# Late modulation blocks in layer 1's mixing, a shorter entry and early zeroing in a two-layer expert-choice transformer kernel

## The chip, the cores and the metric

One core of one Trainium2 chip runs the whole program. The metric is the device time in microseconds (us) of one execution, lower being better; the profiled execution's rows are times from the start of its span.

## The reference, cut to what matters

Two blocks run one behind the other on `x` of 512 tokens by 1024 features; only the first one is touched by the change. It has two layers and carries a second stream of 256 context tokens, `ctx`, that the last layer no longer updates.

```
for i in range(2):
    mods  = silu(c)     @ ada_w[i] + ada_b[i]      # 6 x 1024: sh1, sc1, g1, sh2, sc2, g2
    cmods = silu(c_ctx) @ ada_w[i] + ada_b[i]
    h  = rms_norm(x, n1)  * (1 + sc1) + sh1        # and hc from xc with cmods
    p  = h @ w_in[i]                               # 11 pieces: a_b a_c a_h b_v b_g c_q c_k c_v d_q d_k d_v
    x  = x + g1 * (concat(conv(a), conv31(b), window_attn(c), global_attn(d)) @ w_out[i])
    h2 = rms_norm(x, n2) * (1 + sc2) + sh2
    aff = softmax(h2 @ router)                     # each of 16 experts takes its best 64 (32) tokens
    x  = x + g2 * sum over experts of gate * ((silu(xs @ w_gate) * (xs @ w_up)) @ w_down)
```

All data is float32. A layer's expert weights are 16 x 3 matrices of 1024 x 1024 (4 MB each), its modulation weights `ada_w[i]` 1024 x 6144 (24 MB).

## The kernel before, in words

**Modulation.** `ada_gen` (lines 310 to 332) works `ada_w` off in blocks of 512 output columns, twelve a layer. A block is four loads of 512 KB from the SP queue (`ada_load`, line 191), 8 matmuls into one PSUM bank, a copy on ACT, four transposes, and a reduce and an add on DVE into `M[l]`. Blocks 0 and 1 are sh1, 2 and 3 sc1 (an even block holds features 0 to 511, the odd one the rest), 4 and 5 g1, 6 and 7 sh2, 8 and 9 sc2, 10 and 11 g2. While one block is computed, three or four loads of the next are issued.

**Entry** (lines 211 to 398). The SP queue gets small rows of constants, four loads of `x`, blocks 0, 2, 1 and 3 of layer 0, two loads of `ctx`, and weights for the first dense units. The small rows land in `rows`, are transposed in four groups (`rows_to_cols`, line 347) and become `cols`. Each of six token tiles is squared, transposed and scaled. When all four blocks are there, `norm1_first` (line 387) goes over the eight feature tiles k: ACT makes the rounded part `hh`, DVE the full value and its remainder `hl` (POOL the remainder of the context).

**Dense** (line 419) multiplies with `w_in` and `w_out`: a unit is 128 output columns; its 512 KB of weights are split into a rounded part `wh` (ACT, line 442) and a remainder `wl` (POOL, line 443), and 24 matmuls of 512 columns and, in layer 0, 24 of 256 follow (lines 473, 475), three for each k. The q pieces have their columns regrouped, so `colload2` (line 490) fetches a unit in two loads of 64-column pieces. A unit's weights go through one of five buffers named `raw`, which the modulation loads share. `la` units are loaded ahead, or, with `ahead`, one from a certain unit on.

**Mixing.** `run_all` (lines 944 to 947) weaves four generators: `gd` (18 dense units), `at` (attention), `ga` (modulation blocks) and `cv` (the 31-tap convolution). In layer 0 `ga` makes layer 0's blocks 4 to 11 and layer 1's 0 to 7. In layer 1 it is empty. Attention's rope takes sine and cosine from `tabl`, loaded by POOL's queue (line 638) when the entry's buffers are free.

**Experts** (line 1022). `wload` issues 512 KB weight tiles in the order g0, u0, g1, d0, u1, g2 and so on, into a ring of 25 in layer 0 (18 `rawA`, 5 `raw`, 2 `rawB`). Ahead of layer 0's experts stand the router stage's steps: logits to affinities, writing normalised rows to `hd` in DRAM, eight rounds of max, index and replace on DVE, indices, and the first gathers by POOL (line 1209). Woven into it are layer 1's modulation blocks 8 to 11 (line 1110) and the zeroing of the DRAM sums `sumx` and `sumc` (lines 1134 to 1139). Expert e's outputs are then added to these sums by indirect DMAs, up to e = 13 for x and 11 for the context; the rest goes through one-hot matmuls. Back they come as six tiles `rb` (two buffers), each taken up by two `sums_add` (line 1311) of four transposes and four DVE operations. Context's four stand in expert 15's up product, x's eight in its down product.

**Order.** The code is traced, and a scheduler then orders each engine's instructions by priority, dependencies and free buffers, so the order on an engine is near to the code's, but not the same. Each engine runs its list in order, and so does each DMA queue's issue.

Of the kernel before, what the change touches and what calls it, by code (L numbers as in the profile page):

```python
# [134 lines left out]
def main_kernel(ctx, tc, I, out, stop=None, dbg=None, manual=False):  # L135
# [37 lines left out]
    dx = pool(ctx, "dx", space=DRAM).tile([128, 8 * 768], F32)  # L173
# [44 lines left out]
    rows = ent.tile([128, 4, 128], F32)  # L218
    xin = xip.tile([128, 4, 1024], F32)
    cin = xip.tile([128, 2, 1024], F32)  # L220
    ada0 = ent.tile([128, 4, 4, 1024], F32)
# [20 lines left out]
    x_load(1)  # L242
    row_load(G, 0, "qn", I["q_norm_g"], 2, dup=True)
    row_load(G, 0, "kn", I["k_norm_g"], 2, dup=True)
    row_load(G, 0, "cbb", I["conv_b_b"].rearrange("l (h p) -> (l h) p", p=128), 4)
    row_load(G, 0, "lng", I["conv_ln_g"].rearrange("l (h p) -> (l h) p", p=128), 4)
    row_load(G, 0, "lnb", I["conv_ln_b"].rearrange("l (h p) -> (l h) p", p=128), 4)
# [3 lines left out]
    x_load(2)  # L251
    SY.dma_start(sinkb, bass.AP(tensor=I["sink"].tensor, offset=I["sink"].offset, ap=[[0, 128], [1, 8]]))
    row_load(SY, 0, "fg", I["final_g"].rearrange("(k p) -> k p", p=128), 8)
    row_load(SY, 0, "ln1", I["ln1_2"].rearrange("l (k p) -> (l k) p", p=128), 8)
    x_load(3)
# [3 lines left out]
    ada_load(0, 0, ada0[:, 0], hfs=(0, 1))  # L259
    row_load(SY, 3, "cq", I["conv_qkv_2"].rearrange("l t (h p) -> (l t h) p", p=128), 48)  # L260
    row_load(SY, 3, "fc", I["ffn_conv_2"].rearrange("l t (h p) -> (l t h) p", p=128), 66)
    ada_load(0, 0, ada0[:, 0], hfs=(2, 3))
    ada_load(0, 2, ada0[:, 2])
    for t in range(2):
        SY.dma_start(cin[:, t, :], I["ctx"][0, t * 128:(t + 1) * 128, :])
    ada_load(0, 1, ada0[:, 1])
    pre0 = {}
    pre0[0] = raw_tile().rearrange("p (k c) -> p k c", k=8)
    SY.dma_start(pre0[0], I["w_in"][0, :, 1536:1664].rearrange("(k p) c -> p k c", p=128))
    pre0[1] = raw_tile().rearrange("p (k c) -> p k c", k=8)  # L270
    for h in range(2):
        SY.dma_start(pre0[1][:, :, 64 * h:64 * h + 64],
                     I["w_in"][0, :, 1280 + 128 * h:1344 + 128 * h].rearrange("(k p) c -> p k c", p=128))
    ada_load(0, 3, ada0[:, 3])
# [34 lines left out]
    def ada_gen(l, blocks, pl, psp):  # L309
        g, o, n = RO["adab"]  # L310
        for b in blocks:
# [8 lines left out]
            if 3 < b < 11 or (l == 1 and b != 7 and b < 11):  # L320
                ada_load(l, b + 1, hfs=range(4 if l == 1 and b > 7 else 3))
# [10 lines left out]
            yield  # L332

# [7 lines left out]
    if True:  # L341
        with ExitStack() as e0:
# [4 lines left out]
            def rows_to_cols(g, n):  # L347
                p = pse.tile([128, 512], F32, name="rc")
                T.transpose(p[:, :n], rows[0:n, g, :], ident[0:n, 0:n])
                V.tensor_copy(cols[:, g, 0:n], p[:, :n])  # L350

            rows_to_cols(0, 16)
            A.activation(s2[:, :, 0], col("c"), AF.Silu)
            A.activation(s2[:, :, 1], col("cc"), AF.Silu)
            ga = ada_gen(0, (0, 2, 1, 3), sqp, pse)
            ss = ent.tile([128, 6], F32)
            for t in range(6):
# [16 lines left out]
                if t == 1:  # L374
                    rows_to_cols(1, RO["n", 1])
# [4 lines left out]
            for g in (0, 2, 3):  # L380
                rows_to_cols(g, RO["n", g])
            V.tensor_scalar(nsink, sinkb, -1.0, None, op0=OP.mult)

        entry.close()

        def norm1_first(sqp):
            a1 = sqp.tile([128, 8, 2], F32, name="a1")
            for k in range(8):
# [32 lines left out]
        def dense(units, hh, hl, dw, dps, la=3, pre={}, ahead=None):  # L421
# [5 lines left out]
            def load(i):  # L427
                if i in pre:
                    raw[i] = pre[i]
                elif i < len(units):  # L430
                    raw[i] = raw_tile().rearrange("p (k c) -> p k c", k=8)
                    units[i][0](raw[i])

            def split(i):
                if i < len(units):
                    nk = units[i][4] if len(units[i]) > 3 else 8
                    hi[i] = []
                    for a in range(0, nk, 4):
                        n = min(4, nk - a)
                        wh = dw.tile([128, 4, 128], F32R, name="wh")  # L440
                        wl = dw.tile([128, 4, 128], F32R, name="wl")
                        A.activation(wh[:, :n], raw[i][:, a:a + n], AF.Copy)  # L442
                        G.tensor_tensor(wl[:, :n], raw[i][:, a:a + n], wh[:, :n].bitcast(F32), op=OP.subtract)  # L443
                        hi[i].append((wh, wl))
# [40 lines left out]
        def colload(src, c0, n=128):  # L485
            def f(raw):
                SY.dma_start(raw[:, :, 0:n], src[:, c0:c0 + n].rearrange("(k p) c -> p k c", p=128))
            return f

        def colload2(src, ca, cb):  # L490
            def f(raw):
                for h, c in enumerate((ca, cb)):
                    SY.dma_start(raw[:, :, 64 * h:64 * h + 64], src[:, c:c + 64].rearrange("(k p) c -> p k c", p=128))
            return f
# [107 lines left out]
        def layer(l):  # L602
# [6 lines left out]
            with (es_l0 if has else ExitStack()) as es, ExitStack() as er:  # L609
# [5 lines left out]
                psp = Psum(ps, {"px": 3, "s": 2, "pt": 1, "misc": 1, "y": 1}, {"pc": "px"})  # L615
                if has:

                    hh, hl = hh0, hl0
                    norm1_first(sqp)
# [245 lines left out]
                c0 = dict(a_b=0, a_c=256, a_h=512, b_v=768, b_g=1024, c_q=1280, c_k=1536, c_v=1664,  # L865
                          d_q=1792, d_k=2048, d_v=2176)

                def unit(n, ev, nt=NT, j=0):
                    return (colload(w_in, c0[n] + 128 * j), ev, nt)

                def qunit(n, ev, j):
                    return (colload2(w_in, c0[n] + 64 * j, c0[n] + 128 + 64 * j), ev, NT)

                u_c = [unit("c_k", ev_rope(partial(put_k, kC)), 768)] + \
                      [qunit("c_q", ev_rope(partial(put_q, qC, j)), j) for j in range(2)] + [unit("c_v", ev_v(vC), 768)]
                u_d = [unit("d_k", ev_dk, 768)] + [qunit("d_q", ev_dq(j), j) for j in range(2)] + \
                      [unit("d_v", ev_v(vD), 768)]
                u_b = [unit("b_g", ev_bg(j), j=j) for j in range(2)] + [unit("b_v", ev_bv(j), j=j) for j in range(2)]
                u_a = [unit("a_c", ev_ac(j), j=j) for j in range(2)] + [unit("a_h", ev_ah(j), j=j) for j in range(2)] + \
                      [unit("a_b", ev_ab(j), j=j) for j in range(2)]  # L880
# [52 lines left out]
                ga = iter(())  # L933
                if has:
# [3 lines left out]
                    ga = ada_rest()  # L938

                gd = dense(u_c + u_b + u_d + u_a, hh, hl, dw, psp, pre=pre0 if has else {}, ahead=4 if has else None)  # L940
                at, cv = att_gen(), conv31()
                w1, w2, w3 = (28, 28, 64) if has else (18, 18, 44)
                run_all((dense_part(gd, 12), 12))
                run_all((dense_part(gd, 12), 12), (steps(at, w1), w1), (steps(ga, 8), 8))
                c1 = 16 if has else 8
                run_all((dense_part(gd, 12), 12), (steps(at, w2), w2), (steps(ga, 8), 8), (steps(cv, c1), c1))
                run_all((gd, 18), (at, w3), (ga, 16), (cv, (42 if has else 21) - c1))
# [74 lines left out]
        def experts(l, rwpA, lg, rbias, a2, nA, nB):  # L1022
# [37 lines left out]
            if has:  # L1060
                ada_load(1, 8)
            with ExitStack() as es:
# [4 lines left out]
                if has:  # L1067

                    accs = dr.tile([1024, 512], F32, name="sumx"), dr.tile([1024, 256], F32, name="sumc")
# [16 lines left out]
                with ExitStack() as e2:  # L1086
# [3 lines left out]
                    ga = ada_gen(1, range(8, 12), mp, Psum(ps, {"yx": 1}, {"misc": "yx"})) if has else iter(())  # L1090
# [29 lines left out]
                    for _ in steps(ga, 2):  # L1120
                        pass
# [12 lines left out]
                    if has:  # L1134
                        zz = sqp.tile([128, 1024], F32, name="ht", bufs=4)
                        G.memset(zz, 0.0)
                        for acc_, n in zip(accs, (512, 256)):
# [6 lines left out]
                    for i in range(8):  # L1144
# [5 lines left out]
                        if i in (2, 4, 6):  # L1150
                            for _ in steps(ga, 2):
                                pass
# [827 lines left out]
```

## Time and profile before

| | us |
|---|---|
| median of 3 runs | 2653.49 (2650.05 to 2656.85) |
| the profiled execution | 2657.17 |
| its span, first to last instruction | 2655.0 |

TensorE is busy for 2476.4 us of the span (93%), DVE for 1092.9, ACT for 870.2, POOL for 637.8. The DMA engines are full in two long stretches, the expert stages of the two layers (some 380 to 409 GB/s), and at the entry. Busy TensorE is not TensorE at its peak, and the shares are averages over stages with different limits, so a stage is read by what its waits end on.

### The profile page before, as it was taken

To read this page: it belongs to the slowest core of one execution; us is meant where nothing else is said; L and a number is where in the kernel's file an instruction comes from. 1 tells how busy PE (TensorE), PEld (TensorE's weight loads), DVE (VectorE), ACT (ScalarE), POOL (GpSimd) and SP (SyncE) were. 2 spreads that over 40 slices of the span, in tenths; PEclk is the share of its full clock that TensorE was granted. 3 is DMA by queue.
4 is the path that set the end of the run, shared out by engine and by line. 5 is a ranking of instruction groups with operands and counts; after the bars stand their busy time and mean duration, and the time that the engine had idled before them with its cause. 6 is when DMAs were issued, how large, how long until landed. Compare 5 with 4: busy or idle time off the path is not lost.

```text
span 2655.0 us, 41308 instructions
## 1 busy us (share of the span) xinstructions
PE 2476.4 (93%) x16415; PEld 1500.4 (57%) x16415; DVE 1092.9 (41%) x2371; ACT 870.2 (33%) x1769; POOL 637.8 (24%) x552
## 2 busy tenths in 40 slices
PE   7999999699999999899979989898899999999998
PEld 4766777344444333577753322132577787888886
DVE  4488852311111113689641102021665555444411
ACT  4544362211111110464531111110562435443422
POOL 3533112011111100633220000000333233444443
PEclk8999999899999999799989999999899999999999
DMA  8454455999999998222179999999421102333332
GB/s 281 140 165 139 149 177 197 322 383 385 385 386 385 388 394 313 58 59 52 61 289 386 394 398 399 399 404 409 130 67 32 40 25 64 95 96 96 92 96 67
DMA packets 324758, 584.08 MB, mean 220 GB/s; under 512 B 36864, under 2 KB 190007, under 8 KB 323927
## 3 DMA queue, kind: packets, MB, share of 16 engines
q1 hardware_dynamic: 311943, 555.16, 57.7%
q0 software_dynamic: 12480, 26.23, 4.1%
q8 instruction: 129, 2.11, 0.3%
q14 instruction: 62, 0.51, 0.1%
q10 hardware_dynamic: 144, 0.08, 0.0%
HBM read 556.74 MB, written 18.87 MB: 217 GB/s over the span
## 4 chain that ended last, share of the span: by engine, by line
PE 62%; DMA 21%; DVE 9%; issue 3%; POOL 2%; ACT 1%; SPq 1%; ACTq 0%; DVEq 0%; POOLq 0%
PE px L473 21%; DMA rawA<-in_w_gate_dram 4%; DMA rawA<-in_w_down_dram 4%; PE ax L1243 3%; DMA rawA<-in_w_up_dram 3%; PE yx L1243 3%; PE ux L1243 3%; PE g L473 2%; PE s L553 2%; PE y L584 2%; PE px L475 2%; DMA rawB<-in_w_gate_dram 2%; PE pt L565 2%; PE ac L1248 2%; PE pt L473 2%
## 5 line engine op out<-in xcount | busy, mean ns | idle before, releaser
L443 POOL TENSOR_TENSOR wl<-raw,wh 128x512 fp32r<-128x512 f32 (+1 forms) x312 | 408.2, 1311 | 962.0 <-ACT wh L442 768.1
L442 ACT ACTIVATE wh<-raw 128x512 fp32r<-128x512 f32 (+1 forms) x312 | 193.6, 625 | 441.2 <-PE px L473 211.0
L473 PE MATMUL px<-hh,wh 128*128 128x512 f32 x768 | 315.7, 412 | 6.4 <-DVE xT L1401 1.8
L473 PE MATMUL px<-hh,wl 128*128 128x512 f32 x768 | 313.1, 408 | 6.6 <-POOL wl L443 6.6
L473 PE MATMUL px<-hl,wh 128*128 128x512 f32 x768 | 314.6, 410 | 3.8 <-DVE hl L1019 1.9
L1225 ACT ACTIVATE xt<-tr,mod,a 128x64 f32<-128x64 f32 x256 | 86.9, 405 | 295.5 <-PE tr L1221 285.1
L473 PEld LDWEIGHTS px<-hh,wh 128*128 128x128 f32 x768 | 148.7, 194 | 41.2 <-issue 6.1
L473 PEld LDWEIGHTS px<-hh,wl 128*128 128x128 f32 x768 | 148.8, 194 | 39.7 <-POOL wl L443 7.3
L473 PEld LDWEIGHTS px<-hl,wh 128*128 128x128 f32 x768 | 148.7, 194 | 37.5 <-issue 3.8
L1369 DVE SCALAR_TENSOR_TENSOR Yx<-yx,gcol,Yx 64x512 fp32r<-64x512 f32 x36 | 27.0, 750 | 268.7 <-ACT Yx L1368 268.7
L1209 POOL DMA_INDIRECT xg<-hd,gidx x32 | 29.7, 927 | 431.9 <-PE tr L1221 398.3
L785 DVE SCALAR_TENSOR_TENSOR yT<-ub,cols,yT 128x512 f32<-128x512 f32 (+1 forms) x180 | 126.5, 718 | 0.6
L1243 PE MATMUL ax<-rawA,xt 128*32 128x512 f32 x856 | 116.8, 597 | 2.2 <-DMA rawA<-in_w_gate_dram 2.1
L1273 ACT ACTIVATE sa<-ax 128x512 f32<-128x512 f32 x32 | 19.1, 597 | 290.9 <-PE ax L1243 183.1
L1300 POOL DMA_INDIRECT sumx<-ys,place x14 | 22.0, 1571 | 376.5 <-ACT ys L1347 376.5
L1243 PE MATMUL ux<-rawA,xt 128*32 128x512 f32 x800 | 106.1, 594 | 0.1
L1237 PE MATMUL ux<-rawA,xt 128*64 128x512 f32 x328 | 87.3, 611 | 8.1 <-DMA rawA<-in_w_up_dram 8.0
L1237 PE MATMUL yx<-rawA,hT 128*64 128x512 f32 x316 | 81.5, 621 | 11.0 <-DMA rawA<-in_w_down_dram 10.0
L565 PE MATMUL pt<-tab,P 128*128 128x128 f32 x448 | 82.2, 284 | 6.8 <-DVE PT L571 4.3
L1368 ACT ACTIVATE Yx<-yx,gcol 64x512 fp32r<-64x512 f32 x36 | 24.6, 682 | 190.7 <-PE yx L1237 138.4
L1228 DVE TENSOR_SCALAR xt<-tr,a,mod 128x32 f32<-128x32 f32 x128 | 39.0, 310 | 115.0 <-ACT xt L1225 114.5
L1237 PE MATMUL ax<-rawA,xt 128*64 128x512 f32 x316 | 77.7, 612 | 7.6 <-DMA rawA<-in_w_gate_dram 7.2
(593 smaller groups left out, 4895.0 us busy)
## 6 DMA issues: line engine op xcount, KB each, us to landing
rawA<-in_w_gate_dram SPq DMA_DIRECT2D x186, 512.0 KB, 10.4
rawA<-in_w_up_dram SPq DMA_DIRECT2D x182, 512.0 KB, 10.2
rawA<-in_w_down_dram SPq DMA_DIRECT2D x151, 512.0 KB, 10.4
raw<-in_ada_w_dram SPq DMA_DIRECT2D x80, 512.0 KB, 5.7
raw<-in_w_down_dram SPq DMA_DIRECT2D x74, 512.0 KB, 10.2
raw<-in_w_gate_dram SPq DMA_DIRECT2D x62, 512.0 KB, 8.1
raw<-in_w_in_dram SPq DMA_DIRECT2D x56, 512.0 KB, 3.9
raw<-in_w_up_dram SPq DMA_DIRECT2D x55, 512.0 KB, 10.2
```

The costliest lines, as they stand in the source:

```text
L442: A.activation(wh[:, :n], raw[i][:, a:a + n], AF.Copy)
L443: G.tensor_tensor(wl[:, :n], raw[i][:, a:a + n], wh[:, :n].bitcast(F32), op=OP.subtract)
L473: T.matmul(px, lhsT=w[:, k % 4, :], rhs=h[:, k0 + k, 0:512], start=st, stop=sp_)
L475: T.matmul(pc, lhsT=w[:, k % 4, :], rhs=h[:, k0 + k, 512:nt], start=st, stop=sp_)
L553: T.matmul(s[:, :w], lhsT=q, rhs=k, start=(a == 0), stop=(a == len(mm) - 1))
L565: T.transpose(pt[:, (t - a) * 128:(t - a + 1) * 128], P[:, t * 128:(t + 1) * 128], ident)
L584: T.matmul(y[64 * g:64 * g + 64, bi * 128:(bi + 1) * 128], lhsT=vs[g][t], rhs=PTs[i, g][t // 4][:, (t % 4) * 128:(t % 4 + 1) * 128], start ...
L785: V.scalar_tensor_tensor(acc[:, j, o:o + n], src, w, acc[:, j, o:o + n], op0=OP.mult, op1=OP.add)
L1225: A.activation(xt[:, kk, 0:64], p[:, k * NX:k * NX + 64], AF.Identity, bias=M[l][:, 24 + kk, 0:1], scale=a2[:, kk, 0:1])
L1237: T.matmul(px[64 * g:64 * g + 64, :], lhsT=lx(u), rhs=w[:, 512 * hf:512 * hf + 512], start=first, stop=last)
L1243: T.matmul(px[32 * g:32 * g + 32, :], lhsT=lx(u)[:, 32 * (g % 2):32 * (g % 2) + 32], rhs=w[:, 512 * hf:512 * hf + 512], start=first, stop= ...
L1248: T.matmul(pc[32 * g:32 * g + 32, :], lhsT=lc(u), rhs=w[:, 256 * q:256 * q + 256], start=first, stop=last)
```

## The change

- Layer 1's modulation blocks 8 to 11 go from layer 0's router stage to layer 1's mixing: one block in each of the second and third `run_all`, two in the fourth. Layer 1's `dense` uses `ahead=4` as layer 0's does.
- The sums are zeroed in layer 0's mixing, ahead of the first `run_all`, from a `sq` buffer.
- The entry loads x, blocks 0 and 2, the context, the first unit's weights, blocks 1 and 3, the next two units', and then the constants (seven small loads move from POOL's queue to SP's). Norm and the first half of the first unit go over k = 0 to 3 as soon as blocks 0 and 2 are there; blocks 1 and 3, and norm over 4 to 7, come after.
- A q piece's two units are fetched together, as two loads of 512 KB with 1 KB pieces; both units read both buffers.
- Context's sums are loaded behind expert 12 and taken up in expert 14's up product; x's eight `sums_add` are shared between expert 15's up and down products.
- The ring of 25 weight tiles still has its first loads issued in two parts (18, then 7).

```diff
-    ada0 = ent.tile([128, 4, 4, 1024], F32)
+    rows = raw_tile()[:, 0:512].rearrange("p (g c) -> p g c", g=4)
+    entry2 = ExitStack()
+    ada0 = {b: pl.tile([128, 4, 1024], F32, name=f"ada{b}")
+            for pl, bs in ((ent, (1, 3)), (pool(entry2, "ent2", side="right"), (0, 2))) for b in bs}
...
+    for t in range(1, 4):
+        x_load(t)
+    ada_load(0, 0, ada0[0])
+    ada_load(0, 2, ada0[2])
+    for t in range(2):
+        SY.dma_start(cin[:, t, :], I["ctx"][0, t * 128:(t + 1) * 128, :])
+    pre0 = {0: raw_tile().rearrange("p (k c) -> p k c", k=8)}
+    SY.dma_start(pre0[0], I["w_in"][0, :, 1536:1664].rearrange("(k p) c -> p k c", p=128))
+    ada_load(0, 1, ada0[1])
+    ada_load(0, 3, ada0[3])
+    def pair_load(src, c0):
+        ts = [raw_tile(), raw_tile()]
+        for i, t in enumerate(ts):
+            SY.dma_start(t.rearrange("p (k c) -> p k c", k=4),
+                         src[512 * i:512 * i + 512, c0:c0 + 256].rearrange("(k p) c -> p k c", p=128))
+        return ts
+    pre0[1] = pre0[2] = pair_load(I["w_in"][0], 1280)
...
-            ga = ada_gen(0, (0, 2, 1, 3), sqp, pse)
+            ga = ada_gen(0, (0, 2), sqp, pse)
...
+                    norm1_first(range(4), a1)
+                    gd = dense(units, hh, hl, dw, psp, pre=pre0, ahead=4)
+                    next(gd)
+                    drain(ada_gen(0, (1, 3), sqp, psp))
+                    norm1_first(range(4, 8), a1)
+                    entry.close()
...
-                ga = iter(())
+                else:
+                    ga = ada_gen(1, range(8, 12), sqp, psp)
...
+                g1 = 8 if has else 2
+                if has:
+                    for _ in range(2):
+                        next(gd)
+                    for g in (0, 2, 3):
+                        rows_to_cols(psp, "misc", g, RO["n", g])
+                    zz = sqp.tile([128, 512], F32, name="sq")
+                    G.memset(zz, 0.0)
+                    for acc_, n in zip(accs, (8, 4)):
+                        SY.dma_start(acc_.rearrange("(p a) c -> p (a c)", p=128).rearrange("p (b c) -> p b c", c=512),
+                                     zz[:, None, :].to_broadcast([128, n, 512]))
+                run_all((dense_part(gd, 9 if has else 12), 12))
+                run_all((dense_part(gd, 12), 12), (steps(at, w1), w1), (steps(ga, g1), g1))
...
-                    ga = ada_gen(1, range(8, 12), mp, Psum(ps, {"yx": 1}, {"misc": "yx"})) if has else iter(())
...
-                        if i in (2, 4, 6):
-                            for _ in steps(ga, 2):
-                                pass
...
-                            run_gu("u", e, [], sums_add)
+                            run_gu("u", e, [], lambda u: sums_add(u // 2))
+                        elif has and e == 14:
+                            run_gu("u", e, mid, lambda u: sums_add(8 + u // 2))
```

## Rows read from the trace of the kernel before

**Rows 1.** Windows: busy us (instructions) of PE, PEld, DVE, ACT, POOL; clock, DMA share, GB/s

```profile
103.00:383.00 280.00, 269.73 (x1836) 198.75 (x1828) 219.87 (x572) 142.96 (x334) 63.33 (x52) 0.98 0.52 159
...
456.00:502.00 46.00, 26.11 (x154) 12.35 (x153) 25.21 (x107) 13.82 (x22) 4.52 (x28) 0.78 0.79 281
...
542.00:1057.00 515.00, 509.65 (x6006) 204.83 (x6002) 90.25 (x241) 69.59 (x170) 55.47 (x44) 1.00 1.02 380
...
1100.00:1300.00 200.00, 184.12 (x1108) 144.98 (x1108) 159.87 (x358) 110.72 (x250) 83.98 (x71) 0.96 0.24 61
```

**Rows 2.** Timeline of the SP queue at the entry: start, us, what, [wait before]

```profile
23.42 0.77 SPq L269 DMA_DIRECT2D raw<-in_w_in_dram  x1
24.78 9.45 SPq L272 DMA_DIRECT2D raw<-in_w_in_dram  x2
34.27 2.95 SPq L196 DMA_DIRECT2D ada<-in_ada_w_dram  x4
```

**Rows 3.** Timeline of DVE, PE and POOL at the entry, same columns

```profile
31.63 1.28 DVE L372 TENSOR_TENSOR cin<-xcT,rb 128x512 f32<-128x512 f32 x2 [0.48 <-PE rb L307]
...
42.84 3.35 PE L318 MATMUL misc<-ada,s 128*32 128x512 f32 x8 [0.40 <-DMA ada<-in_ada_w_dram]
...
48.15 0.16 DVE L390 TENSOR_SCALAR a<-mod 128x8 f32<-128x8 f32 x1
...
63.97 1.10 POOL L398 TENSOR_TENSOR hl<-cin,hh 128x256 fp32r<-128x256 f32 x1 [0.23 <-DVE cin L397]
...
71.71 1.28 POOL L678 TENSOR_TENSOR sq<-sq,tabl 128x512 f32<-128x512 f32 x1 [2.21 <-DMA tabl<-in_tab_dram]
```

**Rows 4.** Windows of 5 us at the entry; the last columns are DMA share and GB/s

```profile
10.00:15.00 5.00, 3.62 (x17) 2.88 (x16) 3.81 (x9) 4.64 (x11) 0.00 (x0) 1.00 0.91 296
...
20.00:25.00 5.00, 3.69 (x24) 1.00 (x20) 0.36 (x2) 0.60 (x1) 0.00 (x0) 1.00 1.05 406
...
30.00:35.00 5.00, 3.11 (x15) 0.57 (x13) 2.04 (x4) 1.03 (x3) 0.00 (x0) 1.00 0.88 241
```

**Rows 5.** The chain of waits in layer 0's router stage: start, us, what

```profile
480.82 15.39 DMA raw<-in_ada_w_dram
```

**Rows 6.** Timelines: first gather and first gate product, layer 0, then layer 1

```profile
485.02 1.00 POOL L1209 DMA_INDIRECT xg<-hd,gidx  x1 [6.65 <-DVE tA L1191]
...
502.24 1.07 PE L1243 MATMUL ax<-rawA,xt 128*32 128x512 f32 x8
...
1384.05 1.24 POOL L1209 DMA_INDIRECT xg<-hd,gidx  x1 [22.89 <-DVE tA L1191]
...
1389.46 8.34 PE L1237 MATMUL ax<-rawA,xt 128*64 128x512 f32 x32
```

**Rows 7.** Timeline of ACT: a row per expert at its gate's end (0, 1, 10, 15)

```profile
520.80 0.60 ACT L1273 ACTIVATE sa<-ax 128x512 f32<-128x512 f32 x1
542.01 0.60 ACT L1273 ACTIVATE sa<-ax 128x512 f32<-128x512 f32 x1 [13.38 <-PE ax L1243]
...
837.66 0.60 ACT L1273 ACTIVATE sa<-ax 128x512 f32<-128x512 f32 x1 [13.37 <-PE ax L1243]
...
1012.89 0.60 ACT L1273 ACTIVATE sa<-ax 128x512 f32<-128x512 f32 x1 [19.68 <-PE ax L1243]
```

**Rows 8.** DMA queues from 520 to 1040 us: packets, MB, share

```profile
q1 hardware_dynamic: 52921, 187.77, 92.4%
```

**Rows 9.** The chain of waits in layer 0's mixing: one modulation block on PE

```profile
102.84 1.85 PE misc L318 x16
...
110.74 0.44 PE misc L327 x4
```

**Rows 10.** Timeline of PE in expert 15's down product

```profile
1051.57 0.63 PE L1317 MATMUL tr<-tab,rb 128*128 128x128 f32 x4 [2.11 <-DMA rb<-sumx]
```

**Rows 11.** Window of 4 us at the start of layer 1's experts

```profile
1388.00:1392.00 4.00, 3.62 (x14) 1.69 (x16) 0.00 (x0) 2.98 (x9) 0.88 (x1) 0.50 0.27 79
```

**Rows 12.** The page's part 6: modulation loads, KB each, us to landing

```profile
raw<-in_ada_w_dram SPq DMA_DIRECT2D x80, 512.0 KB, 5.7
```

More of the change, by code (lines that the diff above doesn't have):

```diff
@@ L320, in ada_gen @@
             if 3 < b < 11 or (l == 1 and b != 7 and b < 11):
-                ada_load(l, b + 1, hfs=range(4 if l == 1 and b > 7 else 3))
+                ada_load(l, b + 1, hfs=range(3))
             sb = pl.tile([128, 512], F32, name="sq")
@@ L332, in ada_gen, with rows_to_cols @@
             yield
+    def rows_to_cols(psp, name, g, n):
+        p = psp.tile([128, 512], F32, name=name)
+        T.transpose(p[:, :n], rows[0:n, g, :], ident[0:n, 0:n])
+        V.tensor_copy(cols[:, g, 0:n], p[:, :n])
     es_l0 = ExitStack()
@@ L379, in main_kernel, with norm1_first @@
             drain(ga)
[L380 to L388, printed above, removed]
+        entry2.close()
+        def norm1_first(ks, a1):
+            for k in ks:
                 if k % 4 == 0:
@@ L429, in load @@
                     raw[i] = pre[i]
+                elif i < len(units) and len(units[i]) == 6 and units[i][5]:
+                    raw[i] = raw[i - 1]
+                elif i < len(units) and len(units[i]) == 6:
+                    raw[i] = units[i][0]()
                 elif i < len(units):
@@ L863, in ev_ab @@
                     return f
[L865 to L880, printed above, removed]
+                evs += [ev_rope(partial(put_k, kC))] + [ev_rope(partial(put_q, qC, j)) for j in range(2)] + [ev_v(vC)]
+                evs += [ev_bg(j) for j in range(2)] + [ev_bv(j) for j in range(2)]
+                evs += [ev_dk] + [ev_dq(j) for j in range(2)] + [ev_v(vD)]
+                evs += [ev_ac(j) for j in range(2)] + [ev_ah(j) for j in range(2)] + [ev_ab(j) for j in range(2)]
                 def terms(qt, kt, kv, g, n, a, b):
@@ L1133, in experts @@
                     wload(nB - (6 if l else 0))
[L1134 to L1137, printed above, removed]
-                            SY.dma_start(acc_.rearrange("(p a) c -> p (a c)", p=128).rearrange("p (b c) -> p b c", c=1024),
-                                         zz[:, None, :].to_broadcast([128, n // 128, 1024]))
                     vals = hp.tile([80, 64], F32)
@@ L1266, in run_gu @@
                         if each and u % 2:
-                            each(8 + u // 2)
+                            each(u)
                     acc[w, e] = (px, pc)
@@ L1341, in down @@
                         wload(1)
-                        if has and e == 15:
-                            sums_add(u)
+                        if has and e == 15 and u % 2:
+                            sums_add(4 + u // 2)
                     if has and e < 14:
@@ L1460, in experts @@
                         gather(e + 2)
-                        if has and e in (13, 14):
-                            for t in ((4, 5), range(4))[e - 13]:
+                        if has and e in (12, 14):
+                            for t in ((4, 5), range(4))[e // 2 - 6]:
                                 sums_load(t)
```

84 lines of the change are left out of this document (35 added, 49 removed).

## The prediction

> **What bounds the kernel now.** I read the windows by stage first, then, for each stage that the change touches, its timeline and its chain of waits. Layer 0's mixing keeps TensorE busy for 269.73 of 280 us, layer 1's for 184.12 of 200 (DVE 159.87), and layer 0's experts for 509.65 of 515 with the DMA engines full too; the router stage between leaves TensorE 20 of its 46 us idle [rows 1]. So PE work inside a mixing costs nearly its whole time, PE work in the router stage costs only by what it waits for, and layer 0's experts stand between two limits, to be told apart by their pace.
>
> The pace is on ACT's rows, one per expert. From expert 1 to expert 10 the gates end at 542.01 and 837.66: nine steps of 32.85 us, even to the hundredth, as a fixed list of matmuls is [rows 7]. From 10 to 15 it is 175.23 us, 10.98 more than five such steps. The weights move at 187.77 MB in 520 us, 361 GB/s [rows 8]; a tile of 0.524 MB takes 1.452 us and an expert's 24 take 34.85. Thus DMA is 2 us an expert too slow, the ring of 25 tiles covers it until it is drained, and then DMA sets the pace. What fills the ring late therefore comes back as time at the end.
>
> **The entry.** The normalisation starts at 48.15, after the last modulation tile (TensorE takes it at 42.84), and its last piece ends at 63.97 + 1.10 = 65.07, so eight feature tiles take 16.9 us, half of them 8.5 [rows 3].
> - When the last of the four blocks lands: SP spends 9.45 us on two loads of 64-column pieces while block 3 waits behind them, against 0.77 for the unsplit load of the same size [rows 2]. DMA falls from 406 GB/s to 241 in one of the stretches behind it, and among the small constants it runs at 296 [rows 4]. Over 5 us each these two make (165 + 110) x 5 us = 1.4 MB not moved; with the 0.5 MB of split weights, now behind block 3, 1.9 MB or 4.7 us at 406 GB/s. Block 3 lands at about 38.1.
> - From landing to normalisation it took 48.15 - 42.84 = 5.3 us, so the second half starts at 43.4. The first half needs the context, scaled by 31.63 + 1.28 = 32.9 [rows 3]; even without any gain there it ends at 41.4. So four tiles are hidden behind DMA, and the second four end at 43.4 + 8.5 = 51.9: **13 us earlier** than 65.07.
> - Bounds: all stretches at 406 GB/s and the first unit's matmuls well interleaved give up to 18; if TensorE's queue puts the first unit's half ahead of the late blocks, and DVE's second half waits for both, some 4 are left. I take the middle, which each step gives.
> - The constants are 18 loads on SP, seven of them new there, at some 0.4 us each: 7 us on SP between the paired weights and the next unit's, hidden since three units are loaded by then; if not, they cost what the fourth unit is late. `rows` now takes one of the five `raw` buffers until it is transposed: no price for the same reason. The three transposes, copies and the sink's sign only move.
>
> **Zeroing.** 3.1 MB, 7.7 us at 406 GB/s, go from a stage in which DMA is short to one whose DMA share is 0.52 [rows 1]. SP's issue waits for POOL's fill, behind POOL's remainders; queued behind it are the dense loads, covered by those ahead. Cover gone, it is up to 7.7 us: rope already waits 2.21 us for its table [rows 3], and the zeros could delay that. I take nothing; the loss lies in the entry's lower bound.
>
> **Router stage.** Today TensorE waits 15.39 us for a modulation tile [rows 5], with the gathered rows' transposes in order behind it. The gather is issued at 485.02 and the first gate product starts at 502.24. In layer 1, where no such block stands there, the distance is 1389.46 - 1384.05 = 5.4 us [rows 6]. I leave the gather where it is, with 0.6 for the wider rows here: start at 491.0, **11.2 earlier**. The DVE reductions and ACT copies woven into the top-k rounds may give 1 or 2 more.
>
> Expert 0's gate now takes 520.80 - 502.24 = 18.6 us, since two blocks are woven in; eight tiles at the later pace are 8 x 1.369 = 10.95. TensorE will have stood still before it: in layer 1 the window with the first gate products was granted 0.50, the 1.2 GHz level [rows 11], so 1392 - 1389.46 = 2.5 us at half speed lose 1.3. The gate ends at 491.0 + 12.3 = 503.3, another **6.3**.
>
> [...]
>
> **Experts of layer 0.** The ring can now be full when the experts start: no modulation tile holds a `raw` buffer, and 12 MB (four blocks of 2.1 MB, the zeros) are gone from ahead of it. With 25 tiles there, tile 359 is landed 334 x 1.452 = 485 us after the start, and TensorE at its own pace wants it 12.3 + 21.2 (expert 0 to 1, as now) + 14 x 32.85 = 493 after. So the drain just doesn't come before the end: **10 of the 10.98 us** come back; bounds 3 (a ring short by some tiles) and 11.
>
> **The last expert.** One wait of 2.11 us for the sums' load [rows 10] goes, since their buffers come free an expert earlier: **2**. The transposes only move from the last product to the one before it; both belong to TensorE.
>
> **Layer 1's mixing.** Four blocks at 1.85 + 0.44 = 2.3 us on PE [rows 9]: 9.2 us of work into a stage with 8% of idle time [rows 1]. Bounds: 0 if it all falls into the idle 16 us, 13 if the blocks also wait for loads or for the one PSUM bank that they share; nearest is layer 0's mixing, with 16 such blocks and 4% idle, where little was free. I take **+7**. DVE's share is 4 x 0.4 us. The 16 loads meet a DMA at 0.24. Layer 1's experts are limited by their weights, whose first loads only wait for the mixing's end.
>
> **Sum.** -13 - 11.2 - 6.3 - 10 - 2 + 7 = -35.5 us. Against the profiled execution's own 2657.17 that is 2621.7. The median of the runs is 3.7 lower, so I forecast **2618**.
>
> **Rivals.**
> - *A: the entry keeps its end.* TensorE takes its list in order; if the first unit's half product sits ahead of the late blocks, and zeros and table meet on the DMA engines, the 13 us shrink to nothing: 2631. For it: the table's wait and the POOL-bound stretch behind the entry; against: both halves' inputs stand ready by the rows. Chance 0.11.
> - *B: the ring still runs dry.* If the seven late tiles are issued behind the `hd` writes or compete with the first gather, the gather lands late and the end's 10 us stay: with 3 us of the start lost too, 2631. For it: the first loads stay in two parts, and DMA's share is 1.02 [rows 1]. Against: 12 MB less. Chance 0.09.
> - *C: the change doesn't do what it says.* The scheduler orders by its own priorities. If it places the four late blocks at the end of layer 1's mixing, just ahead of the output projection that needs two of them, their loads and 9.2 us of work stand bare: 15 instead of 7, and as much lost at the joins: 2633. Chance 0.06.
> - *D, slower: the five `raw` buffers.* In layer 1's mixing the late blocks' prefetched tiles hold three of five buffers for four units at a time, and weights are fetched just in time. If a unit's load is thereby bare at 5.7 us [rows 12], the 42.5 us of the other terms are used up at the eighth such unit of 18, and from the ninth it is slower by over 0.3%; all 18 would give about 2653 - 42 + 103 = 2714. Against: layer 0's mixing runs 16 blocks and the same units through the same five buffers, with 4% idle. Chance 0.04.
>
> **How the numbers follow.** The forecast has 0.70; its own range is 2606 to 2630. A, B and C end between 2631 and 2633, so a range from 2602 (the better bounds of entry and mixing) to 2634 leaves out D and the tails. A measurement of this kernel can tell some 0.3%, 8 us, from no change. All cases but D are faster by more, unless two of A to C come together with a bad mixing: faster 0.93, same 0.03, slower 0.04.
>
> **What would show it.** Entry: normalisation in two halves, the first during the loads, the last POOL remainder near 52. Router: no wait for modulation tiles; gate products some 6 us behind the first gather. Experts: 32.85 us a step up to expert 15. Layer 1's mixing: four blocks of 2.3 us and a stage longer by 7. The forecast is wrong if the steps stay near 35 us late in layer 0, if the entry's end moves by under 5, or if layer 1's mixing grows by over 15.

## The result, and the profile after

The changed kernel takes **2693.85 us** (median of 4 runs, 2689.41 to 2698.36) against 2653.33 for the kernel before beside it: a ratio of 1.0152, with a 95% interval of 1.0133 to 1.0172. It is slower, and the forecast of 2618 and its range up to 2634 are missed by far. The profiled execution's span is 2695.4 us, 40.4 longer than before. Taken apart at five marks (the logits' copy at the mixing's end, the gates of [rows 7], the first scatter product, layer 1's first gate), the spans of four kernels differ from before's like this, in us; e1, e2 and e7 are explained below.

| stage | forecast | after | e1 | e2 | e7 |
|---|---|---|---|---|---|
| up to the end of layer 0's mixing | -13 | -3.7 | -5.0 | -13.7 | -13.8 |
| from there to expert 0's gate | -17.5 | -18.4 | -19.9 | -16.8 | +2.1 |
| expert 0's gate to expert 15's | -10 | **+51.1** | -2.6 | -2.1 | +5.5 |
| expert 15's gate to the first scatter | -2 | +0.5 | -6.5 | -6.5 | -5.1 |
| scatter to layer 1's first gate | +7 | +9.9 | +10.2 | +8.0 | +1.8 |
| the rest | 0 | +1.1 | -2.8 | -2.7 | -1.0 |
| sum | -35.5 | +40.4 | -26.6 | -33.8 | -10.5 |

In the changed kernel the loss stands in one stage. Its windows, with the columns of [rows 1], for layer 0's mixing, the router stage and layer 0's experts: in the experts TensorE is idle for 33 of 515 us where it was for 5, and the DMA engines move 353 GB/s where they moved 380.

```profile
103.00:383.00 280.00, 267.47 (x1819) 198.27 (x1818) 219.51 (x557) 140.36 (x328) 62.82 (x51) 0.98 0.51 158
456.00:502.00 46.00, 31.61 (x268) 17.20 (x271) 24.03 (x105) 14.78 (x26) 2.81 (x3) 0.74 0.55 191
515.00:1030.00 515.00, 481.82 (x5519) 204.46 (x5521) 73.69 (x198) 64.80 (x162) 53.89 (x41) 0.98 0.97 353
```

Expert 0's gate comes 22 us earlier than in [rows 7], expert 15's 29 us later. ACT's rows of the gates of experts 0, 1 and 15:

```profile
498.65 0.60 ACT L1285 ACTIVATE sa<-ax 128x512 f32<-128x512 f32 x1
...
529.22 0.60 ACT L1285 ACTIVATE sa<-ax 128x512 f32<-128x512 f32 x1 [22.77 <-PE ax L1255]
...
1041.79 0.60 ACT L1285 ACTIVATE sa<-ax 128x512 f32<-128x512 f32 x1 [17.83 <-PE ax L1255]
```

What TensorE waits for is plain in its timeline: again and again a product on a `raw` tile, 37 to 40 us apart, which is one round of the ring of 25 places at steps of some 36 us.

```profile
559.46 1.06 PE L1255 MATMUL ax<-raw,xt 128*32 128x512 f32 x8 [1.40 <-DMA raw<-in_w_gate_dram]
...
596.84 1.06 PE L1255 MATMUL ax<-raw,xt 128*32 128x512 f32 x8 [2.19 <-DMA raw<-in_w_gate_dram]
...
636.47 1.93 PE L1255 MATMUL ax<-raw,xt 128*32 128x512 f32 x8 [2.87 <-DMA raw<-in_w_gate_dram]
...
673.49 1.06 PE L1255 MATMUL yx<-raw,hT 128*32 128x512 f32 x8 [0.57 <-DMA raw<-in_w_down_dram]
```

A gap that comes back every round, on the engine that should be full: the Trainium skill (*Perfetto Trace Analysis*, section "Identifying Performance Opportunities", its part on optimization strategy) says that such consistent bubbles can mean that there isn't enough memory for the next tile to be allocated. Here a tile indeed gets no buffer, though not for want of memory: the buffers exist and are held. SP's waits from 490 to 1070 us (engine and line, releaser: us in total, times, longest) show it. In the changed kernel SP stands up to 10.9 us, which is eight tiles at TensorE's 1.369 us a tile, until TensorE has used up an earlier tile; with the buffers free it is 1.9 at most (e1, below).

```profile
SPq L1083 <- PE yc L1260: 98.7, 49, 9.9
...
SPq L1083 <- PE ac L1260: 62.9, 29, 8.1
...
SPq L1083 <- PE uc L1260: 43.8, 34, 10.9
```

The holder is the helper of the modulation blocks, in a line that the change left as it was but for the number of tiles. After block 7 of layer 1, at the end of layer 0's mixing, it loads three tiles of block 8 ahead into `raw` buffers. Before, block 8 was computed in the router stage, from 462 us on. Now it is computed in layer 1's mixing, and until then three of the five `raw` buffers are held; with two left, the ring's third `raw` place waits until the tile of its first has been used up. SP's rows show the last modulation loads of layer 0's mixing and then two weight tiles for `raw`, where the list has five; TensorE reads block 8 only at 1158.70:

```profile
337.79 29.55 SPq L199 DMA_DIRECT2D raw<-in_ada_w_dram  x8
...
433.35 8.83 SPq L1083 DMA_DIRECT2D raw<-in_w_gate_dram  x2
```

```profile
1158.70 1.92 PE L326 MATMUL misc<-raw,s 128*32 128x512 f32 x16
```

### The profile page after: what moved, and what is told of

Its sections match the earlier page's. It is cut to its first block, busy times and chain, and to the rows that moved or that the text cites. A ratio compares the mean times of both kernels' runs of the same rounds, so it can differ in the third digit from the quotient of the medians.

```text
span 2695.4 us, 41094 instructions
## 1 busy us (share of the span) xinstructions
PE 2482.9 (92%) x16415; PEld 1515.1 (56%) x16415; DVE 1095.6 (41%) x2371; ACT 869.0 (32%) x1769; POOL 633.1 (23%) x545
## 4 chain that ended last, share of the span: by engine, by line
PE 67%; DMA 20%; DVE 8%; POOL 2%; issue 2%; ACT 1%; SPq 0%; ACTq 0%; DVEq 0%; POOLq 0%
PE px L486 20%; PE ax L1255 4%; PE yx L1255 4%; DMA rawA<-in_w_down_dram 4%; PE ux L1255 4%; DMA rawA<-in_w_gate_dram 3%; PE g L486 2%; PE px L488 2%; PE y L591 2%; PE s L560 2%; DMA raw<-in_w_down_dram 2%; PE ac L1260 2%; DMA rawA<-in_w_up_dram 2%; PE yc L1260 2%; PE uc L1260 2%; PE pt L572 2%
## 5 line engine op out<-in xcount | busy, mean ns | idle before, releaser
L1255 PE MATMUL ux<-rawA,xt 128*32 128x512 f32 x800 | 124.4, 593 | 0.0
L1293 DVE TENSOR_TENSOR sa<-ux,sa 128x512 f32<-128x512 f32 x32 | 22.1, 692 | 180.9 <-PE ux L1255 77.5
```

Source lines behind the costliest of these rows:

```text
L1255: T.matmul(px[32 * g:32 * g + 32, :], lhsT=lx(u)[:, 32 * (g % 2):32 * (g % 2) + 32], rhs=w[:, 512 * hf:512 * hf + 512], start=first, stop= ...
```

## The experiments

The kernel before was run beside each; its medians in the four comparisons were 2653.33, 2653.47, 2654.42 and 2655.02. Ratios are to it.

**e1: no tile of block 8 fetched at the end of layer 0's mixing.** One condition of the changed kernel:

```
-            if 3 < b < 11 or (l == 1 and b != 7 and b < 11):
+            if (3 < b < 11 and (l, b) != (1, 7)) or (l == 1 and b != 7 and b < 11):
```

> The changed kernel, but the modulation helper doesn't fetch three tiles of layer 1's block 8 at the end of layer 0's mixing. Theory H (held buffers: these three tiles sit in three of the five raw buffers through all of layer 0's experts, so that the ring of 25 weight tiles has two raw buffers where it counts on five): the gates of experts 1 to 15 come 32.85 us apart, expert 15's near 980 us instead of 1041.79, layer 1's first units no longer wait for buffers, and the time is 2625 to 2640. Rival R (weights come slower for another reason: the sums' loads and adds moved, the paired loads, the zeros): steps stay near 36 us, 2685 to 2700.

Measured: 2630.04 us (2626.27 to 2634.5), ratio 0.9909 [0.9885, 0.9933]. That line alone is worth 64 us. SP loads three modulation tiles fewer, and five weight tiles for `raw` instead of two:

```profile
334.71 18.92 SPq L199 DMA_DIRECT2D raw<-in_ada_w_dram  x5
...
410.08 13.53 SPq L1083 DMA_DIRECT2D raw<-in_w_gate_dram  x3
...
431.81 8.85 SPq L1083 DMA_DIRECT2D raw<-in_w_gate_dram  x2
```

SP's longest wait for TensorE in L1083, from 490 to 1070 us as above, falls to 1.9:

```profile
SPq L1083 <- PE uc L1260: 27.1, 40, 1.9
SPq L1083 <- PE ac L1260: 23.3, 33, 1.8
```

Theory H holds for the time, but the steps are even only up to expert 12, and expert 15's gate comes at 985.39 instead of near 980.

**e3: the kernel before with nothing but the late blocks**, tiles of block 8 held as in the change:

```
-                    ga = ada_gen(1, range(8, 12), mp, Psum(...)) if has else iter(())
+                    ga = ada_gen(1, range(8, 12), sqp, psp)
...
-                run_all((gd, 18), (at, w3), (ga, 16), ...)
+                run_all((gd, 18), (at, w3), (ga, 16 if has else 4), ...)
```

> The kernel before with one part of the change: blocks 8 to 11 of layer 1 in layer 1's mixing, with the prefetch of three tiles across layer 0's experts as the change has it. Theory H: it loses nearly all that the changed kernel loses: steps near 36 us from expert 0 to 15, 2685 to 2705. Rival R: steps of 33 to 35 us as before, 2635 to 2655.

Measured: 2695.09 us (2692.0 to 2699.45), ratio 1.0159 [1.0136, 1.0182]. One part of the change, with the tiles held, loses as much as the whole change; the entry has no share in the loss.

**e5: the tiles held, but the ring's list without the places they take.** In layer 0 `raw` stands twice instead of five times:

```
-            slots = ["A"] * nA + ["W"] * 5 + ["B"] * nB
+            slots = ["A"] * nA + ["W"] * (2 if has else 5) + ["B"] * nB
...
-                wload(5 if has else 0)
+                wload(2 if has else 0)
```

> The changed kernel with the three tiles of block 8 still held through layer 0's experts, but with the list of places for the experts' weights changed: in layer 0 the `raw` buffers stand in it twice instead of five times, so that the ring has 22 places, all of them free. The output is unchanged. Theory P (places): the 59 us that the held tiles cost layer 0's experts come from the three places in the list whose buffer isn't there: reading ahead falls there to two tiles, once every 25 tiles. With 22 true places the loss is three tiles of 1.45 us at the end, 4 us: 2628 to 2642. Theory C (contention): the loss comes from the tiles and transfers as such, wherever the places are: 2680 to 2700.

Measured: 2641.85 us (2637.71 to 2648.58), ratio 0.9957 [0.9946, 0.9968]: at the upper edge of theory P and far from C. Same tiles held, same bytes moved, 52 us back: most of the time is lost not to the held memory, but to a list that goes on counting with it. Against e1, 11.8 us remain from gate 0 to gate 15, not the 4 expected; e9 bears on where the rest comes from.

**e2 and e4: where the sums are zeroed.** e2 is e1 with the zeroing back in the router stage, as before; e4 is e1 with it in layer 0's mixing, ahead of the fourth group of units instead of the first. The diff is e4's.

```
                 V.tensor_scalar(nsink, sinkb, -1.0, None, op0=OP.mult)
-                    zz = sqp.tile([128, 512], F32, name="sq")
...
                 run_all((dense_part(gd, 9 if has else 12), 12))
...
                 run_all((dense_part(gd, 12), 12), (steps(at, w2), w2), (steps(ga, g1), g1), (steps(cv, c1), c1))
+                if has:
+                    zz = sqp.tile([128, 512], F32, name="sq")
...
```

> As e1_release, and the sums are zeroed where they were before, in layer 0's router stage. Theory Z (the zeros' 3.1 MB and the sq buffer that they hold take back most of the entry's lead of 16 us between 63 and 107 us): layer 0's mixing ends some 8 us earlier than in e1_release, the router stage takes at most 3 us more, and the time is 3 to 10 us below e1_release. Rival (the lead is lost anyway in the stretch from 150 to 280 us, where DVE is busy for 45 of 50 us): same as e1_release, or up to 5 us slower.

> As e1_release, with the zeros ahead of the fourth group of layer 0's mixing, near 200 us. Theory Z: the entry's lead is kept to that point, 3 to 10 us below e1_release, and no more than 3 us from e2_zeros_back. Rival (lead lost anyway): same as e1_release within 3 us.

Measured: e2 2626.44 us (2623.07 to 2629.06), ratio 0.9898 [0.9877, 0.9919]; e4 2626.91 (2623.18 to 2630.63), 0.9894 [0.9871, 0.9918]. Both sizes are as expected, but the intervals overlap e1's, so the medians alone don't show a gain; the traces have to. The mixing ends at 444.45 in e2, 453.16 in e1. Single traces differ at this mark, so all count: with the zeros early it is 450.12 to 454.44 (the changed kernel, e1, e5), with the zeros in the router stage 442.94 to 449.76 (e2, e6 to e9), 452.6 and 445.5 on average. On these averages the zeros cost the mixing some 7 us. What happens behind the entry is on the chain of the changed kernel: the partition move of the second q unit takes 7 us.

```profile
72.82 0.50 POOL qC L692
73.33 1.23 POOL sq L704
74.56 7.03 DMA qC<-sq
```

The issues from 55 to 95 us (KB each, median us from issue to landing), the changed kernel first, then e2, without the 3 MB of zeros in this stretch:

```profile
sumx<-sq SPq DMA_DIRECT2D x1, 2048.0 KB
...
sumc<-sq SPq DMA_DIRECT2D x1, 1024.0 KB
...
kC<-kC POOLq DMA_DIRECT2D x2, 256.0 KB, 8.6
qC<-sq POOLq DMA_DIRECT2D x4, 128.0 KB, 4.4
kC<-kC POOLq DMA_DIRECT2D x2, 128.0 KB, 2.9
qC<-sq POOLq DMA_DIRECT2D x4, 64.0 KB, 5.9
```

```profile
kC<-kC POOLq DMA_DIRECT2D x2, 256.0 KB, 3.5
qC<-sq POOLq DMA_DIRECT2D x4, 128.0 KB, 2.4
kC<-kC POOLq DMA_DIRECT2D x2, 128.0 KB, 6.4
qC<-sq POOLq DMA_DIRECT2D x4, 64.0 KB, 3.2
```

Of the small moves that sit between rope and the first scores, three groups take about twice as long beside the zeros, and the fourth, `kC` of 128 KB, less than half as long. The first `kC` group (8.6 to 8.8 in the changed kernel, e1 and e5, 3.4 to 3.8 in e2, e4, e6 and e7) and the last `qC` group (4.7 to 5.9, and 2.3 to 3.2) differ in all of these traces. That these moves carry the loss is argued from the chain, not shown apart. The DMA share was 0.52 over the whole mixing [rows 1], but here it is 0.82 to 0.95, first in the changed kernel and then in e2:

```profile
60.00:75.00 15.00, 13.57 (x76) 11.37 (x75) 4.51 (x9) 5.11 (x10) 14.42 (x15) 1.00 0.82 257
...
75.00:90.00 15.00, 8.95 (x50) 7.18 (x48) 4.78 (x12) 5.98 (x11) 8.90 (x11) 0.90 0.95 222
```

```profile
60.00:75.00 15.00, 11.71 (x54) 9.93 (x55) 6.88 (x9) 4.94 (x10) 14.02 (x13) 0.89 0.69 173
...
75.00:90.00 15.00, 12.01 (x72) 10.04 (x71) 5.13 (x7) 5.28 (x10) 12.41 (x14) 1.00 0.37 87
```

In e2 the zeros stand ahead of weights in the router stage instead and take 3.1 us back there (the table's second line, against e1).

**e7: e2 with the late blocks back in the router stage**, that is the change without late blocks and early zeroing. The edit's main lines:

```
-                    ga = ada_gen(1, range(8, 12), sqp, psp)
+                    ga = iter(())
...
+                        if i in (2, 4, 6):
+                            for _ in steps(ga, 2):
+                                pass
```

> The release with the zeroing back in the router stage, and with the late modulation blocks back there too: of the change the paired entry loads, the halved first norm and the layout of the last expert's sums are left. The output is unchanged. Theory L: the late blocks are worth what the forecast said of the router stage and the ring, less what they cost layer 1's mixing. Layer 1's mixing gets 8 us shorter (338 to 340 us from the scatter to layer 1's first gate), the gather 10 to 15 later against the mixing's end, gate 0 some 17: 2626.4 + 17 - 8 = 2632 to 2640. Theory N: they are worth nothing, since the ring takes back at the end what the router stage gave: 2618 to 2628.

Measured: 2643.57 us (2639.18 to 2647.89), ratio 0.996 [0.9947, 0.9972]: theory L and more than it. So the late blocks without the held tiles make 0.62% or 17 us. TensorE waits for their tiles again, as in [rows 5]:

```profile
PE yx L326 <- DMA raw<-in_ada_w_dram: 15.0, 3, 14.3
```

Gate 0 comes 18.8 us later than in e2, layer 1's mixing is 6.2 shorter. Expected were 17 and 8. The 17 us aren't all the blocks' own: from gate 0 to gate 15 e7 takes 7.6 us more than e2, with less waiting for weights and a worse order of transposes, which e6 and e9 explain.

**e6: e2 with a ring of 21 places.** `((18, 2), (20, 8))` becomes `((14, 2), (20, 8))`.

> The release with the zeroing back in the router stage, and a ring four places shorter (21 instead of 25) in layer 0's experts. The output is unchanged. Theory R (the ring is drained): from expert 0's gate to expert 15's it took 490.0 us with 25 places, 9 more than fifteen steps at TensorE's own pace, because the weights come at 1.45 us a tile. With four places fewer the drain comes earlier and four tiles of 1.45 us more are lost: 495 to 497 for the distance, about 2632 for the run. Theory S (the sums' loads and the last experts' other traffic cost the 9 us, and the ring isn't drained before): the distance stays at 490 to 491.5, the run at 2625 to 2628.

Measured: 2640.27 us (2634.37 to 2641.7), ratio 0.9948 [0.9927, 0.9968]; gate 0 to gate 15 takes 499.5. The first step longer than 32.85 is that to expert 10's gate, in e2 that to expert 12's, as a drained ring asks, but 9.5 us are more than the 5.8 of theory R, and neither theory gives 499.5. Expert 15's step alone takes 40.06 us, in e5 40.07, in e7 40.07: so even a figure points to a list of matmuls, not to a transfer, and PE's rows in this step show no wait for weights. In these three kernels the scheduler set the transposes of the last two or three steps between the products one or two at a time. The kernel before has such a list too. From its timeline of PE between the gates of experts 12 and 13:

```profile
915.62 0.39 PE L1221 MATMUL tr<-tab,xg 96*128 96x96 f32 x2
...
917.37 0.39 PE L1221 MATMUL tr<-tab,xg 96*128 96x96 f32 x2
...
919.11 0.30 PE L1221 MATMUL tr<-tab,xg 96*128 96x96 f32 x1
```

In e1 and e2 the eight stand in a row up to the end. From e2's timeline:

```profile
754.38 1.04 PE L1256 MATMUL ux<-rawA,xt 128*32 128x512 f32 x8
...
755.67 1.04 PE L1256 MATMUL ux<-rawA,xt 128*32 128x512 f32 x8
...
757.08 0.88 PE L1234 MATMUL tr<-tab,xg 96*128 96x96 f32 x8
757.89 1.07 PE L1256 MATMUL ux<-rawA,xt 128*32 128x512 f32 x8
```

A tile takes 755.67 - 754.38 = 1.29 us, one with eight transposes behind it 757.89 - 755.67 = 2.22, so they cost 0.93.

**e9: that price by itself.** e2 with the eight transposes of gathered rows set one by one between the up products, for every expert.

```
+                            if k < 3:
+                                yield
...
+                        next(iter(gx), None)
```

> The release with the zeroing back in the router stage, and the eight transposes of each expert's gathered rows set one by one between the eight products of the up matrix, instead of eight in a row; nothing else of layer 0's experts is changed, and the output is unchanged. Theory O (the order in TensorE's list has a price): in the traces a transpose by itself between two products makes the distance from tile to tile 1.66 us instead of 1.29, eight in a row make it 2.22. Eight alone cost 8 x 0.37 - 0.93 = 2.0 us more an expert: steps of 34.9 instead of 32.85, nothing left for the weights to be late, 511 to 515 us from expert 0's gate to expert 15's instead of 490.0, and 2646 to 2654 for the run. Theory W (the longer tiles were hidden waits for weights, and the order is free): the steps stay at 32.85 until the weights are late, the distance at 489 to 492, the run at 2622 to 2630.

Measured: 2651.58 us (2649.18 to 2657.43), ratio 0.9989 [0.9978, 1.0], 25 us more than e2. The steps are 34.86 us from expert 1 on (expected 34.9), gate 0 to gate 15 takes 513.8. Theory O holds on every number. A tile and its transpose in e9's timeline, and the start of the next:

```profile
701.41 1.06 PE L1263 MATMUL ux<-rawA,xt 128*32 128x512 f32 x8
702.29 0.61 PE L1268 MATMUL uc<-rawA,xt 128*32 128x256 f32 x8
702.84 0.30 PE L1238 MATMUL tr<-tab,xg 96*128 96x96 f32 x1
703.07 1.06 PE L1263 MATMUL ux<-rawA,xt 128*32 128x512 f32 x8
```

The tile takes 703.07 - 701.41 = 1.66 us: a lone transpose costs 0.37, one of a row of eight 0.12. This takes before's last five steps apart. From expert 10 to 15 they are 10.98 us too long; tile distances beyond these prices, which are waits for weights, make 3.4 of it (most of it at 893 to 900 us), and the scattered transposes 7.5. The same count gives e5's remainder over e1: 4.1 us of waits, near what the three missing places ask (4.4), and 7.7 of scattered transposes. For e6 it gives 5.8 us of waits against e2's 5.4, hardly any of the extra ones that theory R asked for, as would follow if the slower list lets the weights catch up; with the list changed as well, e6 doesn't decide between its theories. For e7 it gives 4.1. What made the scheduler choose either list wasn't tried.

**e8 and e10: layer 1's query weights unit by unit; and the best of all.** e8 is e2, e10 is e4, both with this:

```
+                        if n[2] == "q" and l == 1:
+                            units.append((colload2(w_in, c0[n] + 64 * j, c0[n] + 128 + 64 * j), ev, nt))
```

> The release with the zeroing back in the router stage, and layer 1's two pairs of query weights loaded as before the change, each unit by itself in 64-column pieces; layer 0 keeps the pairs. The output is unchanged. Theory Q: of the 8 us that layer 1's mixing is longer than before, the pairs cost 2, since each wants two of the five `raw` buffers at once while block 8 holds four: 344 to 345 us from the scatter to layer 1's first gate, the run at 2623 to 2625. Theory B: the late blocks cost all 8, and the distance stays at 346 to 347; if the 64-column pieces cost more than the pairs, it grows.

> What beat both kernels so far, put together: the release, the zeroing ahead of the fourth group of units in layer 0's mixing, layer 1's query weights loaded unit by unit. The output is unchanged. If the two small gains add (3.5 from the zeroing, 2 to 3 from the unpaired loads): 2622 to 2626. If the zeroing only moves the loss from the router stage to the mixing, as the two places that were tried gave the same time: no better than with the zeroing in the router stage, 2621 to 2626 too, with the mixing's end 3 us later and gate 0 to gate 15 no shorter than 490.

Measured: e8 2623.17 us (2621.52 to 2627.64), ratio 0.9896 [0.9877, 0.9916]; e10 2623.71 (2617.15 to 2627.54), 0.9877 [0.9858, 0.9896]. From scatter to layer 1's first gate it is 344.0 in e8 against e2's 346.4, both numbers as theory Q has them, but 346.9 in e10 against e4's 346.7, and e6 has 345.3 with the pairs: theory Q isn't borne out, and what makes the 2 us of layer 1's mixing beyond the late blocks stays open. e2, e4, e8 and e10 can't be told apart by their intervals; all beat both kernels, by 1.0 to 1.2% against before and 2.5 to 2.6% against the change.

## Why the prediction was wrong

**The step that failed** is the first sentence on layer 0's experts: "The ring can now be full when the experts start: no modulation tile holds a `raw` buffer". It follows the consumer, which is gone from the router stage, and not the producer, which isn't: the load ahead at block 7 stands where it stood. Of the 75.9 us between 2693.85 and 2618, 64 are this line (e1). Rival D named the resource, the five `raw` buffers held by prefetched tiles, but looked for it in layer 1's mixing, where the same holding costs little; its chance of 0.04 and the range left the true place out. The thing to see it by stood in the kernel: the place list of the ring has the `raw` buffers in it, and SP takes that list in order. The prediction's own sign of being wrong, steps near 35 us late in layer 0, came true: from gate 1 on the changed kernel's steps are 31.5 to 42.9 us, 36.6 on average.

**The entry: earlier, by how much is not settled, and then eaten.** Without the zeroing the mixing ends 13.7 us earlier (e2), against -13, but the agreement is in part luck. e3, whose code up to this mark is that of the kernel before, ends its mixing at 450.93, 7.2 us before the profiled execution of that kernel (458.18). From 40 to 440 us the two were granted a clock of 0.95 and 0.97 (the column behind POOL's), first the kernel before, then e3:

```profile
40.00:440.00 400.00, 380.64 (x2394) 286.00 (x2392) 266.67 (x652) 181.32 (x400) 119.73 (x105) 0.95 0.56 173
```

```profile
40.00:440.00 400.00, 381.24 (x2436) 287.41 (x2431) 269.31 (x655) 182.96 (x403) 119.86 (x105) 0.97 0.55 173
```

On the averages of the traces, 454.6 for these two and 445.5 for the five with the zeros back, the entry is worth some 9 us of the 13. The norm itself gained less than forecast, its last piece being ready at 53.6 in e2 and 56.4 in the changed kernel, where 51.9 was forecast and 65.07 was the time before [rows 3] (62.85 in e3). The zeroing, which was taken as nothing with up to 7.7 should its cover be gone, cost some 7 (8.7 between e1 and e2, 453.16 against 444.45): the mixing's mean share hid a full stretch at its start. As a net effect on the run the medians of e1 and e2 differ by 3.6 with overlapping intervals; the router stage loses 3.1 when the zeros are there.

**Router stage and expert 0's gate: right.** -17.5 was forecast, -18.4 measured in the changed kernel; its first gate product starts 6.3 us behind the first gather (478.37), where 6.0 was forecast. TensorE's first products came at half speed, as priced, but two tiles of them:

```profile
484.69 1.94 PE L1255 MATMUL ax<-rawA,xt 128*32 128x512 f32 x8
...
487.25 1.93 PE L1255 MATMUL ax<-rawA,xt 128*32 128x512 f32 x8
...
489.76 1.03 PE L1255 MATMUL ax<-rawA,xt 128*32 128x512 f32 x8
```

The distances are 2.56 and 2.51 us and then 1.29, so 2.5 are lost instead of 1.3; the window from 484 to 488 us was granted 0.50, the 1.2 GHz level, and that from 492 to 496 1.00. TensorE had stood idle for 7.75 us until the gathered rows came. The Trainium skill's rule against idle gaps between bursts of matmuls (*TensorE: Matmul & The Clock Gate*, "Why this matters for your kernels") agrees with that. The gather is now what the stage waits for, 9.7 us of TensorE's time in e2.

**The ring at the end: the cause was half wrong.** "10 of the 10.98 us come back" took all of it for late weights. Only 3.4 were; 7.5 were transposes set apart (e9). In e1 and e2 the transposes stand in rows, and 4.8 and 5.4 us of waits for weights take their place. ACT's gates of experts 12 to 15 in e1:

```profile
878.39 0.60 ACT L1285 ACTIVATE sa<-ax 128x512 f32<-128x512 f32 x1 [13.37 <-PE ax L1255]
...
915.15 0.60 ACT L1285 ACTIVATE sa<-ax 128x512 f32<-128x512 f32 x1 [17.27 <-PE ax L1255]
...
948.89 0.60 ACT L1285 ACTIVATE sa<-ax 128x512 f32<-128x512 f32 x1 [13.62 <-PE ax L1255]
...
985.39 0.60 ACT L1285 ACTIVATE sa<-ax 128x512 f32<-128x512 f32 x1 [16.30 <-PE ax L1255]
```

878.39 to 915.15 is the wait for weights, 36.76 instead of 32.85, and 0.9 more follow in the next step. The last step is no wait: it takes 36.50 us in e1, e2, e4, e8 and e10 alike, since the context's four `sums_add` now stand in it. One of their groups of transposes in e1:

```profile
962.09 0.66 PE L1329 MATMUL tr<-tab,rb 128*128 128x128 f32 x4
```

In e1 16 of the 48 such transposes stand ahead of gate 15, in the kernel before four. So most of these 3.65 us are work that the change moved over the mark, out of the last expert's line of the table into the ring's, and the two lines are best read together: 9 us came back of 12.

The forecast let the weights run from the start at 1.452 us a tile. In e1 DMA moved only 264 GB/s from 480 to 500 us, while the full ring waited for TensorE to free places, and then 384 from 600 to 700, which is 1.365 us a tile: 1.452 was an average and not a limit. Why the weights still come late at experts 13 and 14 stays open.

**Layer 1's mixing: right.** The late blocks cost 6.2 us (e2 against e7) and 6.4 (e3 against before), against +7; in the changed kernel and e1 the stage is 10 longer, and what the other 2 to 4 are stays open (e8, e10); kernels with the same layer 1 differ among themselves (8.0 in e2, 7.0 in e6, 8.1 in e9).

**Rivals A, B and C** didn't come: the entry's end moved, the ring ran dry late and by little once it had its places, and the late blocks are spread over layer 1's mixing (1158.7 to 1301.8 us in the changed kernel). With the held line undone, e1 is 12 us over the forecast. By the table 8.9 of them are the terms: 8.0 for the mixing's end, 7.4 for the ring and 3.2 for layer 1's mixing are too much, and the other three stages give 9.7 back. The other 3.1 are the median's distance to the span, which is 1.6 above in e1 and was 1.5 below in the kernel before.

## What to carry to other kernels

When a consumer is moved, look for what is still fetched for it at its old time: a tile that waits in a shared pool holds its buffer through every stage in between, and a list of buffers that is taken in order then stalls at the held place, however many others are free. A transfer's cover is the DMA share of the stretch that it lands in, not of its stage. Before a slow tail is put down to transfers, compare the engine's own list there with that of an even step. And one trace a kernel doesn't settle a stage's gain to a few us: the granted clock differs between executions, so set kernels with the same stage side by side.

## What the runs showed of the hardware

- A 96-column transpose alone between two groups of 16 products lengthened their distance by 0.37 us, eight in a row by 0.93. The Trainium skill (*TensorE: Matmul & The Clock Gate*, "Part 4: PE-mode transpose") gives some 390 ns for one of 128x128 in bf16 alone and 275 in a kernel, near the first figure though another size and type; that eight in a row cost 0.12 each is what these runs add.
- Beside 3 MB of zeros being written, partition moves of 256 and 64 KB landed in 8.6 and 5.9 us (changed kernel) instead of 3.5 and 3.2 (e2); those of one group of 128 KB landed sooner, in 2.9 instead of 6.4.
- A full ring delays DMA: e1's engines moved 264 GB/s from 480 to 500 us, where SP waited for TensorE to free a place until 485.93, and 384 from 600 to 700.
- Two executions with the same code up to the end of layer 0's mixing (the kernel before and e3) were granted a clock of 0.95 and 0.97 from 40 to 440 us and reached it at 458.18 and 450.93.
